# Two model blocks on one core: the second block's attention emitted in three stages per half head, across heads

## The chip, the cores and the metric

The kernel runs as one program on one core of a Trainium2 chip. The metric is the device time of that program in microseconds (us): the median of repeated runs. One further execution was recorded by the profiler. The rows shown in this document come from that recording, and their times count from the start of its span.

The engines are called PE (matrix engine; PEld is its loading of weights), DVE (vector), ACT (scalar activations), POOL (general) and SP (it issues the DMAs here).

## What is computed

The reference has two parts. The first (`first_block`, two layers of feed-forward, a mixer and feed-forward) is not touched by the change. The second is two layers of the function below, on 512 tokens of width 1024, with 16 heads of size 64:

```python
def hybrid_layer(x, mem, norm_g, w_in, w_out, mem_norm_g, w_mem_kv, qk_g):
    h = rms_norm(x, norm_g)
    proj = jnp.einsum('btd,de->bte', h, w_in)
    sizes = [D_MOBA] * 4 + [D_DIL] * 4 + [D_MEM] * 2
    cuts = [int(c) for c in np.cumsum(sizes)[:-1]]
    a_q, a_k, a_v, a_g, b_q, b_k, b_v, b_g, m_q, m_g = jnp.split(proj, cuts, axis=-1)

    qa = rope(rms_norm(to_heads(a_q, N_HEADS_MOBA), qk_g[0]))
    ka = rope(rms_norm(to_heads(a_k, N_HEADS_MOBA), qk_g[1]))
    oa = from_heads(moba_attention(qa, ka, to_heads(a_v, N_HEADS_MOBA)))
...
    ob = from_heads(dilated_attention(qb, kb, to_heads(b_v, N_HEADS_DIL)))

    mkv = jnp.einsum('bmd,de->bme', rms_norm(mem, mem_norm_g), w_mem_kv)
    m_k, m_v = jnp.split(mkv, 2, axis=-1)
...
    om = from_heads(memory_attention(qm, km, to_heads(m_v, N_HEADS_MEM)))

    y = jnp.concatenate([oa * jax.nn.silu(a_g), ob * jax.nn.silu(b_g), om * jax.nn.silu(m_g)], axis=-1)
    return x + jnp.einsum('bte,ed->btd', y, w_out)
```

There are 6, 6 and 4 heads of the three kinds, and 256 memory rows. With 512 tokens the kernel computes the first two kinds of attention as causal attention with one table added to the scores (a causal mask for a; for b a mask with the logarithm of how many of the patterns hold a key). Memory attention has no mask and 256 keys.

## The kernel before

*Precision.* Every operand of a matmul is held as two tiles, a rounded one (h, made on ACT by `hi`) and the residue (l, made by `lo` on DVE or POOL), and a product is three matmuls (`mm3`, lines 56 to 58). Weights come by DMA as `wf` and are split into `wh` and `wl`, three pieces ahead.

*Order.* The program is handed to a planner (`TileContext(nc, schedule_with_timeline_sim=True)`), which lays out each engine's instructions ahead of time along a modelled timeline. The order of emission is the priority; `high_priority(offset=n)` moves a stretch n instructions forward. An instruction whose operands or buffers are not free in the model lets later ones go first. On the chip each engine then runs its list strictly in that order, and waits where an operand is late. What is told below of places and order is the order of emission.

*Buffers.* Tiles with the same tag share a number of buffers. In PSUM: `acc` 3, `sc` 2 (scores), `tp` 2 (transposes), `o` 1 (weighted sums). In SBUF: `p` 3 (exponentials), `t` 6 (a scratch ring shared by `os`, `rx`, `sq`, `u`, `n`, `m`, `th`, `mf`, `mss`), `AH2`, `AL2`, `AH4`, `AL4` one each, `qk` 2, `v` 2, `gate` 4.

*A layer of the second block* (`hyb`). Eight pairs of heads are attended in the order of `PAIRS`; pairs 6 and 7 are the memory heads. Beside pair number pos the part `HYB[1 + pos]` is emitted as fill: u projects q and k of a pair (4 steps), v values of four heads (4), g a gate (2), m the memory's keys and values (4), and A, B, C are quarters of the output projection (4 each). `HYB[0]` comes ahead of the first pair, the last quarter behind the last. `blend` (line 569) steps through `attend` and after its i-th yield brings the fill up to the share i/n of its steps. Behind a unit u the products are turned into the layout of q and k by `turned`, two steps later.

*The attention of a pair* (`attend`, line 832 on). A pair has two heads h, and a head two halves (token blocks 0, 1 and 2, 3). For one half head:

- `scores` (838, 839): two matmuls for each block of 128 queries into `sc`; both blocks share a tile in the first half and for memory pairs, otherwise each has its own;
- `softmax` (824 to 829): on DVE the table is added and the minimum taken (scores are negated), on ACT the exponential with its sum into `l8`;
- transposes of `p` through `tp` (877 and 899), then `AH` on ACT and `AL` on DVE;
- `weighted` (846, 848): AH times (vh, vl) and AL times vh, accumulated in `po` (tag `o`). After the second half the two parts of `po` are added into `osum` (ACT, then DVE 912).

These four are emitted in one run. There is a yield behind each half and one between the two blocks of a second half, so a pair has 7 yields, and 5 in memory pairs. At a pair's end come 1/l (`rl` 915, `rx` 917, four transposes `pr` 920), two products with the gate (922, 923) and the split into `yh` and `yl`, which the output projection reads. A pair is finished before the next begins.

Of the kernel before, what the change touches and what calls it, by code (L numbers as in the profile page):

```python
# [11 lines left out]
F = _mybir.dt.float32  # L12
# [33 lines left out]
class Kernel:  # L46
# [532 lines left out]
    def hyb(self, l, hp, stats, after, late):  # L579
# [251 lines left out]
        def attend(pair, k):  # L831
# [20 lines left out]
            for h in range(2):  # L852
                head = 2 * pair + h
                hi_ = slice(64 * h, 64 * h + 64)
                po = self.ps.tile([P, T], F, tag="o", name="o", bufs=1)
                for half in range(2):
                    blocks = [(2 * half + ii, 2 if mem else 2 * half + ii + 1) for ii in range(2)]
                    if half == 0 or mem:
                        nb = sum(kn for _, kn in blocks)
                        sc = self.ps.tile([P, T], F, tag="sc", name="sc", bufs=2)  # L860
                        p = hp.tile([P, T], F, tag="p", name="p", bufs=3)
                        pt = self.ps.tile([P, T], F, tag="tp", name="pt", bufs=2)
                        o = 0
                        for i, kn in blocks:
                            e = o + kn * P
                            scores(sc[:, o:e], h, i, kn * P, o == 0, e == nb * P)
                            o = e
                        o = 0
                        for i, kn in blocks:
                            softmax(head, i, sc[:, o:o + kn * P], p[:, o:o + kn * P], l8[:, i, h:h + 1])  # L870
                            o += kn * P
                        o = 0
                        for i, kn in blocks:
                            for kt in range(kn):

                                to = kt * 2 + i % 2 if nb == 4 else kt + i
                                nc.tensor.transpose(pt[:, to * P:(to + 1) * P], p[:, o:o + P], self.ident)  # L877
                                o += P
                        AH = hp.tile([P, T], R, tag="AH2", name="AH", bufs=1)
                        AL = hp.tile([P, T], R, tag="AL2", name="AL", bufs=1)  # L880
                        n = nb * P
                        self.hi(AH[:, :n], pt[:, :n])
                        self.lo(nc.vector, AL[:, :n], pt[:, :n], AH[:, :n])
                        c = 256 * half
                        parts = [(0, slice(c, c + 256), AH[:, 0:256], AL[:, 0:256], half == 0, False),
                                 (1, slice(c + 512 - n, c + 256), AH[:, 256:n], AL[:, 256:n], False, half == 1)]
                    else:

                        AH = hp.tile([P, 7, P], R, tag="AH4", name="AH", bufs=1)
                        AL = hp.tile([P, 7, P], R, tag="AL4", name="AL", bufs=1)  # L890
                        for i, kn in blocks:
                            n = kn * P
                            sc = self.ps.tile([P, T], F, tag="sc", name="sc", bufs=2)
                            p = hp.tile([P, T], F, tag="p", name="p", bufs=3)
                            scores(sc[:, :n], h, i, n, True, True)
                            softmax(head, i, sc[:, :n], p[:, :n], l8[:, i, h:h + 1])
# [6 lines left out]
                            if i == 2:  # L903
                                yield
                        parts = [(3, slice(384, 512), AH[:, 0], AL[:, 0], False, False)]
                        for kt in range(3):
                            A = [A[:, 2 * kt + 1:2 * kt + 3].rearrange("p a b -> p (a b)") for A in (AH, AL)]
                            parts.append((kt, slice(256, 512), *A, False, kt == 2))
# [286 lines left out]
```

## Time and profile before

| | |
|---|---|
| median of 3 runs | 2488.4 us (2486.3 to 2491.72) |
| the profiled execution | 2487.4 us |
| its span, from first to last instruction | 2485.6 us |
| PE busy | 2419.5 us, 97% of the span |
| the second block | from about 1842 us to the end |

A busy time is a union of the recorded spans of an engine's instructions. Matmuls are pipelined and their recorded spans overlap, so PE that is busy all the time isn't PE at its peak. The granted clock (PEclk) is the share of the matrix engine's full clock; a mean of 0.89 over a stretch means that part of it ran at half the clock. A row of the list of waits says who waited, for whom, the sum of the idle time of the waiting engine in us, how often, and the longest.

### The profile page before, as it was taken

Reading aid. Unit: us, or ns where it says so; the run is one execution under the profiler, and the core shown is the slowest. Engines: PE = TensorE matmul, PEld = TensorE weight load, DVE = VectorE, ACT = ScalarE, POOL = GpSimd, SP = SyncE. Lnnn points to the kernel's source line nnn. Section 1 sums busy time; section 2 is a strip of 40 time slices with the busy share of each in tenths; the row PEclk is TensorE's granted clock in tenths of the full one; section 3 lists DMA queues with packets and bytes.
Section 4 is the critical chain, followed back from the end, with each engine's and each line's share of the span. In section 5 each row is a group of like instructions: output and inputs, shape, how many; then the busy total and the mean of one; then the engine's idle time right before and its main releaser. Section 6 shows DMA issues by size and latency. Waiting matters only on the chain.

```text
span 2485.6 us, 32583 instructions
## 1 busy us (share of the span) xinstructions
PE 2419.5 (97%) x12278; PEld 2046.9 (82%) x12278; DVE 968.8 (39%) x1721; ACT 1071.3 (43%) x2029; POOL 1305.0 (53%) x1018
## 2 busy tenths in 40 slices
PE   8999999999999999999999999999998999899998
PEld 6888888887888888888888888888887899788987
DVE  3111014773111011111115771111037688967888
ACT  4333335544333233333335653333345566555664
POOL 7676555537677556667556447766653122231121
PEclk9999999999999999999999999999999999989999
DMA  3332333222323333333332223333332221122212
GB/s 129 93 102 94 95 100 97 84 78 87 102 93 98 98 94 98 98 95 99 95 107 91 80 77 94 96 100 94 100 108 73 89 68 60 60 77 85 69 60 77
DMA packets 66975, 223.36 MB, mean 90 GB/s; under 512 B 7681, under 2 KB 10881, under 8 KB 66817
## 3 DMA queue, kind: packets, MB, share of 16 engines
q1 hardware_dynamic: 66816, 221.27, 28.7%
q8 instruction: 97, 1.59, 0.3%
q14 instruction: 62, 0.50, 0.1%
HBM read 219.14 MB, written 2.10 MB: 89 GB/s over the span
## 4 chain that ended last, share of the span: by engine, by line
PE 87%; DVE 8%; issue 2%; ACT 2%; POOL 2%; DMA 1%; SPq 0%; POOLq 0%; DVEq 0%; ACTq 0%
PE acc L56 20%; PE acc L57 20%; PE acc L58 20%; PE up L56 6%; PE up L58 6%; PE up L57 6%; DVE wl L67 1%; POOL ss L126 1%; PE sc L838 1%; PE o L846 1%; PE sc L839 1%; PE o L848 1%; DVE x L194 1%; DVE xl L114 1%; PE pt L877 1%
## 5 line engine op out<-in xcount | busy, mean ns | idle before, releaser
L67 POOL TENSOR_TENSOR wl<-wf,wh 128x512 fp32r<-128x512 f32 (+1 forms) x654 | 834.8, 1277 | 661.1 <-ACT wh L62 655.5
L62 ACT CAST wh<-wf 128x512 fp32r<-128x512 f32 (+1 forms) x814 | 497.5, 612 | 1110.4 <-PE acc L57 686.6
L56 PE MATMUL acc<-xh,wh 128*128 128x512 f32 x992 | 389.6, 393 | 6.5 <-ACT wh L62 6.0
L57 PE MATMUL acc<-xl,wh 128*128 128x512 f32 x992 | 389.4, 392 | 6.0 <-DVE xl L114 5.8
L58 PE MATMUL acc<-xh,wl 128*128 128x512 f32 x992 | 388.0, 391 | 0.1
L57 PE MATMUL up<-xl,wh 128*128 128x512 f32 x704 | 274.1, 389 | 0.0
L56 PE MATMUL up<-xh,wh 128*128 128x512 f32 x704 | 274.1, 389 | 0.0
L58 PE MATMUL up<-xh,wl 128*128 128x512 f32 x704 | 273.9, 389 | 0.0
L56 PE MATMUL acc<-hh,wh 128*128 128x512 f32 x704 | 273.9, 389 | 0.0
L57 PE MATMUL acc<-hl,wh 128*128 128x512 f32 x704 | 273.9, 389 | 0.0
L58 PE MATMUL acc<-hh,wl 128*128 128x512 f32 x704 | 273.9, 389 | 0.0
L57 PEld LDWEIGHTS acc<-xl,wh 128*128 128x128 f32 x992 | 186.7, 188 | 47.2 <-DVE xl L114 10.4
L57 PE MATMUL acc<-wl,xh 128*128 128x256 f32 (+1 forms) x752 | 220.7, 295 | 3.8 <-DVE wl L67 3.8
L56 PEld LDWEIGHTS acc<-xh,wh 128*128 128x128 f32 x992 | 186.8, 188 | 45.5 <-ACT wh L62 6.0
L58 PE MATMUL acc<-wh,xl 128*128 128x256 f32 (+1 forms) x752 | 220.3, 295 | 0.6 <-DVE xl L114 0.6
L56 PE MATMUL acc<-wh,xh 128*128 128x256 f32 (+1 forms) x752 | 216.5, 295 | 2.0 <-DVE v L704 1.6
L58 PEld LDWEIGHTS acc<-xh,wl 128*128 128x128 f32 x992 | 186.5, 188 | 38.3 <-POOL wl L67 0.9
L211 DVE TENSOR_TENSOR u<-up,R 128x512 f32<-128x512 f32 x88 | 60.8, 691 | 387.3 <-PE up L58 387.3
L209 DVE TENSOR_TENSOR g<-acc,R 128x512 f32<-128x512 f32 x88 | 60.9, 692 | 381.5 <-PE acc L58 381.4
L639 POOL TENSOR_TENSOR n<-u,ts 128x512 f32<-128x512 f32 x24 | 33.2, 1386 | 310.7 <-ACT u L635 310.4
L222 DVE SCALAR_TENSOR_TENSOR x<-acc,x 128x512 f32<-128x512 f32 x32 | 22.1, 692 | 389.4 <-PE acc L58 389.4
L58 PEld LDWEIGHTS acc<-hh,wl 128*128 128x128 f32 x704 | 132.1, 188 | 27.5
(235 smaller groups left out, 4372.4 us busy)
## 6 DMA issues: line engine op xcount, KB each, us to landing
wf<-wgu SPq DMA_DIRECT2D x175, 512.0 KB, 3.5
wf<-wdn SPq DMA_DIRECT2D x64, 512.0 KB, 3.5
wf<-w2u SPq DMA_DIRECT2D x28, 512.0 KB, 3.6
wf<-wdn SPq DMA_DIRECT2D x32, 384.0 KB, 3.1
wf<-wmi SPq DMA_DIRECT2D x20, 512.0 KB, 3.5
wf<-wmo SPq DMA_DIRECT2D x16, 512.0 KB, 3.6
wf<-w2g SPq DMA_DIRECT2D x16, 512.0 KB, 3.5
wf<-w2o SPq DMA_DIRECT2D x16, 512.0 KB, 3.5
```

What stands on the lines that cost most here:

```text
L56: mm(out, sh, mh, start=start, stop=False, **kw)
L57: mm(out, sh, ml, start=False, stop=False, **kw)
L58: mm(out, sl, mh, start=False, stop=stop, **kw)
L62: self.nc.scalar.copy(out, src)
L67: eng.tensor_tensor(out, src, hi.bitcast(F), op=ALU.subtract)
L114: nc.vector.scalar_tensor_tensor(xl, self.x[k], g, xh.bitcast(F), op0=ALU.mult, op1=ALU.subtract)
L126: eng.tensor_tensor(self.ss[:, :n], self.ss[:, :n], sq[:, :n], op=ALU.add)
L194: self.nc.vector.tensor_tensor(self.x[d], po, self.x[d], op=ALU.add)
L209: nc.vector.tensor_tensor(g, pg, Rb, op=ALU.mult)
L211: nc.vector.tensor_tensor(u, pu, Rb, op=ALU.mult)
L639: nc.gpsimd.tensor_tensor(by4(n), by4(u), si, op=ALU.mult)
L838: nc.tensor.matmul(sc, q[:, t], kh[:, :n], start=first, stop=False, skip_group_check=True)
```

## The change

A half head is taken apart into three stages. `begin` emits scores and softmax and returns two functions: `turn` (transposes, AH and AL) and `weigh` (the weighted sum, after the second half the sum into `osum`, and after the pair's last unit the gate product and the split). A dictionary `stage` that lives across pairs holds what the unit before left: `advance` calls the transposes of the unit before, yields, then the weighted sum of the one before that, and yields. So there are three yields a unit, 12 a pair, for memory pairs as well. The last unit's `turn` and `weigh` and the last but one's `weigh` are called in the next pair's part. Two more calls of `advance` follow the last pair. 1/l and its product with the gate move from the pair's end into `turn` of its last unit, ahead of its last weighted sum. AH and AL get a tile for the first half and one for the second; memory pairs, which had one for both, alternate. `blend` gets n = 12, and 17 for the last pair, in place of 7, 5 and 9.

```diff
--- before.py
+++ after.py
@@ -849,81 +849,109 @@
             osum = scratch("os")
             l8 = self.sp.tile([P, 4, 2], F, tag="l8", name="l8", bufs=2)
...
+            po = [None]
+            def begin(h, half):
                 head = 2 * pair + h
...
+                blocks = [(2 * half + ii, 2 if mem else 2 * half + ii + 1) for ii in range(2)]
+                both = half == 0 or mem
+                ps_ = []
+                if both:
+                    sc = self.ps.tile([P, T], F, tag="sc", name="sc", bufs=2)
+                    p = hp.tile([P, T], F, tag="p", name="p", bufs=3)
+                    nb = sum(kn for _, kn in blocks)
+                    o = 0
+                    for i, kn in blocks:
+                        e = o + kn * P
+                        scores(sc[:, o:e], h, i, kn * P, o == 0, e == nb * P)
+                        ps_.append((i, kn, sc[:, o:e], p[:, o:e]))
+                        o = e
+                    for i, kn, c, q in ps_:
+                        softmax(head, i, c, q, l8[:, i, h:h + 1])
+                else:
+                    for i, kn in blocks:
+                        n = kn * P
                         sc = self.ps.tile([P, T], F, tag="sc", name="sc", bufs=2)
                         p = hp.tile([P, T], F, tag="p", name="p", bufs=3)
...
+                        scores(sc[:, :n], h, i, n, True, True)
+                        softmax(head, i, sc[:, :n], p[:, :n], l8[:, i, h:h + 1])
+                        ps_.append((i, kn, sc[:, :n], p[:, :n]))
+                parts = []
+                def turn():
+                    AH = hp.tile([P, 4 + 3 * half, P], R, tag=f"AH{half}", name="AH", bufs=1)
+                    AL = hp.tile([P, 4 + 3 * half, P], R, tag=f"AL{half}", name="AL", bufs=1)
+                    if both:
+                        pt = self.ps.tile([P, 4, P], F, tag="tp", name="pt", bufs=2)
+                        for i, kn, _, p in ps_:
                             for kt in range(kn):
                                 to = kt * 2 + i % 2 if nb == 4 else kt + i
...
+                                nc.tensor.transpose(pt[:, to], p[:, kt * P:(kt + 1) * P], self.ident)
+                        self.hi(AH[:, :nb], pt[:, :nb])
+                        self.lo(nc.vector, AL[:, :nb], pt[:, :nb], AH[:, :nb])
                         c = 256 * half
...
+                        A2 = lambda f, t: tuple(flat(A[:, f:t]) for A in (AH, AL))
+                        parts.extend([(0, slice(c, c + 256), *A2(0, 2), half == 0, False),
+                                      (1, slice(c + 512 - nb * P, c + 256), *A2(2, nb), False, half == 1)])
                     else:
...
+                        for i, kn, _, p in ps_:
                             pt = self.ps.tile([P, 4, P], F, tag="tp", name="pt", bufs=2)
                             for kt in range(kn):
                                 nc.tensor.transpose(pt[:, (kt + i - 2) % 4], p[:, kt * P:(kt + 1) * P], self.ident)
                             ah, al = (A[:, 3 - i:7:2] for A in (AH, AL))
                             self.hi(ah, pt[:, :kn])
                             self.lo(nc.vector, al, pt[:, :kn], ah)
...
+                        parts.append((3, slice(384, 512), AH[:, 0], AL[:, 0], False, False))
                         for kt in range(3):
...
+                            parts.append((kt, slice(256, 512), *(flat(A[:, 2 * kt + 1:2 * kt + 3]) for A in (AH, AL)),
+                                          False, kt == 2))
+                    if h == 1 and half == 1:
+                        rl = self.sp.tile([P, 8], F, tag="rl8", name="rl8", bufs=2)
+                        nc.vector.reciprocal(rl, flat(l8))
+                        rx = scratch("rx").rearrange("p (a b) -> p a b", b=64)
+                        nc.vector.tensor_scalar(rx, rl.unsqueeze(2).to_broadcast([P, 8, 64]), 0.5, None, op0=ALU.mult)
+                        pr = self.ps.tile([P, T], F, tag="tp", name="pr", bufs=2)
+                        for i in range(4):
+                            nc.tensor.transpose(pr[:, i * P:(i + 1) * P], flat(rx[:, 2 * i:2 * i + 2]), self.ident)
+                        nc.vector.tensor_tensor(gates[pair], gates[pair], pr, op=ALU.mult)
+                def weigh():
+                    if half == 0:
+                        po[0] = self.ps.tile([P, T], F, tag="o", name="o", bufs=1)
+                    weighted(po[0], h, parts)
                     if half == 1:
...
+                        hi_ = slice(64 * h, 64 * h + 64)
+                        self.hi(osum[hi_], po[0][64:P])
+                        nc.vector.tensor_tensor(osum[hi_], po[0][0:64], osum[hi_], op=ALU.add)
+                        if h == 1:
+                            gt = gates[pair]
+                            nc.vector.tensor_tensor(gt, gt, osum, op=ALU.mult)
+                            y_tile(k)
+                            self.hi(yh[k], gt)
+                            self.lo(nc.vector, yl[k], gt, yh[k])
+                return turn, weigh
+            for h in range(2):
+                for half in range(2):
+                    new = begin(h, half)
                     yield
...
+                    yield from advance(new)
+        stage = {"turn": None, "weigh": None}
+        def advance(new):
+            old, w = stage["turn"], stage["weigh"]
+            if old is not None:
+                old[0]()
+            yield
+            if w is not None:
+                w()
+            stage["turn"], stage["weigh"] = new, old and old[1]
             yield
         def due(n):
@@ -950,9 +978,11 @@
             pass
         for pos, pair in enumerate(self.PAIRS):
             part = self.HYB[1 + pos]
-            n = 5 if pair >= 6 else 7
-            self.blend(attend(pair, pos), n + 2 if pos == 7 else n, steps(part), sum(self.STEPS[c[0]] for c in part.split()))
+            fill, m = steps(part), sum(self.STEPS[c[0]] for c in part.split())
+            main = attend(pair, pos)
+            if pos == 7:
+                main = itertools.chain(main, advance(None), advance(None))
+            self.blend(main, 17 if pos == 7 else 12, fill, m)
             if pos == 1:
                 late()
         for _ in self.out_part(yh, yl, 3, after):
```

## Rows read from the trace of the kernel before

**Rows 1.** Page, part 1: each engine's busy us (share of the span) xinstructions

```profile
PE 2419.5 (97%) x12278; PEld 2046.9 (82%) x12278; DVE 968.8 (39%) x1721; ACT 1071.3 (43%) x2029; POOL 1305.0 (53%) x1018
```

**Rows 2.** Stretches: us, busy of PE, PEld, DVE, ACT, POOL; clock; DMA share, GB/s

```profile
0.00:1842.00 1842.00, 1818.63 (x8319) 1508.46 (x8320) 460.92 (x753) 709.16 (x1238) 1165.79 (x927) 1.00 0.31 95
1842.00:2486.00 644.00, 600.90 (x3961) 538.48 (x3959) 507.86 (x968) 362.18 (x791) 139.18 (x91) 0.97 0.24 74
...
1903.00:1950.00 47.00, 34.60 (x179) 26.64 (x178) 34.18 (x69) 29.37 (x67) 15.14 (x14) 0.89 0.26 79
2220.00:2260.00 40.00, 32.51 (x150) 24.66 (x149) 30.80 (x62) 26.98 (x62) 13.28 (x12) 0.83 0.25 77
...
2430.00:2470.00 40.00, 38.84 (x202) 32.01 (x201) 38.13 (x73) 21.80 (x48) 8.88 (x5) 1.00 0.17 54
2180.00:2220.00 40.00, 40.00 (x302) 38.33 (x302) 27.34 (x55) 21.31 (x47) 9.62 (x6) 0.99 0.26 80
...
2380.00:2400.00 20.00, 16.50 (x107) 14.14 (x106) 15.45 (x36) 11.44 (x31) 6.06 (x4) 0.91 0.03 3
```

**Rows 3.** What PE waited for, 1842 to 2486: us in total, times, longest us

```profile
PE o L846 <- ACT AH L62: 5.2, 7, 1.1
PE acc L56 <- ACT mm L759: 4.8, 3, 2.6
PE o L846 <- DVE os L912: 4.6, 6, 1.4
PE o L848 <- DVE AL L67: 3.9, 6, 2.0
...
PE pr L920 <- DVE rx L917: 2.8, 2, 1.8
PE po L56 <- ACT yh L62: 2.7, 2, 1.4
...
PE pt L877 <- DVE AL L67: 1.5, 1, 1.5
```

**Rows 4.** The same in the memory stretches, 1903 to 1950, then 2220 to 2260

```profile
PE o L848 <- DVE AL L67: 2.0, 1, 2.0
PE o L846 <- DVE os L912: 1.8, 2, 1.4
...
PE o L846 <- ACT AH L62: 1.1, 1, 1.1
PE pr L920 <- DVE rx L917: 1.0, 1, 1.0
...
PE pr L920 <- DVE rx L917: 1.8, 1, 1.8
PE o L846 <- DVE os L912: 1.4, 1, 1.4
PE o L848 <- DVE AL L67: 0.8, 2, 0.4
PE o L846 <- ACT AH L62: 0.3, 1, 0.3
```

**Rows 5.** PE's timeline in the sixth pair: start us, us, instruction, [idle before]

```profile
2069.26 0.34 PE L838 MATMUL sc<-qk 128*128 128x384 f32 x1
...
2069.62 0.28 PE L846 MATMUL o<-AH,v 128*128 128x256 f32 x1
2069.74 0.28 PE L848 MATMUL o<-AL,v 128*64 128x256 f32 x1
```

**Rows 6.** What SP's queue waited for, 1842 to 2486: us, times, longest

```profile
SPq L755 <- DVE gate L814: 9.6, 1, 9.6
SPq L755 <- DVE rx L917: 6.5, 1, 6.5
...
SPq L755 <- DVE gate L923: 4.1, 2, 2.9
```

More of the change, by code (lines that the diff above doesn't have):

```diff
@@ L851, in attend @@
             l8 = self.sp.tile([P, 4, 2], F, tag="l8", name="l8", bufs=2)
-            for h in range(2):
+            po = [None]
+            def begin(h, half):
                 head = 2 * pair + h
[L854 to L859, printed above, removed]
+                blocks = [(2 * half + ii, 2 if mem else 2 * half + ii + 1) for ii in range(2)]
[16 more added lines that the diff above has]
+                        n = kn * P
@@ L860, in attend @@
                         sc = self.ps.tile([P, T], F, tag="sc", name="sc", bufs=2)
                         p = hp.tile([P, T], F, tag="p", name="p", bufs=3)
[L862 to L873, printed above, removed]
+                        scores(sc[:, :n], h, i, n, True, True)
+                        softmax(head, i, sc[:, :n], p[:, :n], l8[:, i, h:h + 1])
+                        ps_.append((i, kn, sc[:, :n], p[:, :n]))
+                parts = []
@@ L878, in attend @@
[L878 to L883, printed above, removed]
+                                nc.tensor.transpose(pt[:, to], p[:, kt * P:(kt + 1) * P], self.ident)
+                        self.hi(AH[:, :nb], pt[:, :nb])
@@ L884, in attend @@
+                        self.lo(nc.vector, AL[:, :nb], pt[:, :nb], AH[:, :nb])
                         c = 256 * half
-                        parts = [(0, slice(c, c + 256), AH[:, 0:256], AL[:, 0:256], half == 0, False),
-                                 (1, slice(c + 512 - n, c + 256), AH[:, 256:n], AL[:, 256:n], False, half == 1)]
-                    else:
[L889 to L896, printed above, removed]
+                        A2 = lambda f, t: tuple(flat(A[:, f:t]) for A in (AH, AL))
@@ L909, in attend @@
-                    weighted(po, h, parts)
-                    if half == 1:
-                        self.hi(osum[hi_], po[64:P])
-                        nc.vector.tensor_tensor(osum[hi_], po[0:64], osum[hi_], op=ALU.add)
-                    yield
-            rl = self.sp.tile([P, 8], F, tag="rl8", name="rl8", bufs=2)
-            nc.vector.reciprocal(rl, flat(l8))
-            rx = scratch("rx").rearrange("p (a b) -> p a b", b=64)
-            nc.vector.tensor_scalar(rx, rl.unsqueeze(2).to_broadcast([P, 8, 64]), 0.5, None, op0=ALU.mult)
@@ L918, in attend @@
-            pr = self.ps.tile([P, T], F, tag="tp", name="pr", bufs=2)
-            for i in range(4):
-                nc.tensor.transpose(pr[:, i * P:(i + 1) * P], flat(rx[:, 2 * i:2 * i + 2]), self.ident)
-            gt = gates[pair]
-            nc.vector.tensor_tensor(gt, gt, pr, op=ALU.mult)
-            nc.vector.tensor_tensor(gt, gt, osum, op=ALU.mult)
-            y_tile(k)
-            self.hi(yh[k], gt)
-            self.lo(nc.vector, yl[k], gt, yh[k])
+                            parts.append((kt, slice(256, 512), *(flat(A[:, 2 * kt + 1:2 * kt + 3]) for A in (AH, AL)),
+                                          False, kt == 2))
```

6 lines of the change are left out of this document (removed).

## The prediction

> **What bounds the kernel now.** I first read the totals of the page: the matrix engine (PE) is busy 97% of the span [rows 1], so only what lets PE idle or slows it can be won. Then the table by stretch [rows 2] splits the span at 1842 us, where the second block begins. Before it PE is busy 1818.6 of 1842.0 us; the change touches nothing there. In the second block it is busy 600.9 of 644.0 us at a mean granted clock of 0.97: 43.1 us idle, and some 0.03 x 644 = 19 us of clock. That is all there is to win, and it is not spread evenly. The stretch 2180 to 2220 shows no idle time. The stretches 1903 to 1950 and 2220 to 2260, where the memory keys and values (the step m) are projected beside the attention of the second pair, lose 12.4 and 7.5 us of PE and run at a clock of 0.89 and 0.83. The stretch 2380 to 2400 loses 3.5 us at 0.91 [rows 2].
>
> Third, the list of what PE waited for in the second block [rows 3]. Five of its rows are waits inside the attention: the weighted sum for its left part AH (5.2 us, 7 times), for the sums of the head before to leave the one buffer o (4.6 us, 6 times), for the residue AL (3.9 us, 6 times), the transposes of 1/l for rx (2.8 us, 2 times), a transpose for a buffer that AL had still to read (1.5 us, once). Together 18.0 us in 22 waits. They are the target. The same list for the two memory stretches alone [rows 4], with the one transpose wait of 1.5 us, which stands in the first of them, holds 7.4 us in 6 waits and 4.3 us in 5: 11.7 us in 11 of the 22. So only 6.3 us in 11 waits lie anywhere else.
>
> The rows understate a wait a little. A weighted matmul is shown as 0.28 us long, but in an unbroken run the next one starts 0.12 us after it [rows 5]. The record runs 0.16 us past the moment at which the next could have started, so I add 0.16 us to each wait.
>
> **The change, part by part.** It adds and removes no instruction and no transfer. The same scores, exponentials, transposes, AH, AL and weighted sums are emitted in another order, and an order of emission is all that the planner gets from the program. Before, a half head was emitted as one run (scores, softmax, transposes, AH and AL, weighted sum) with fill between half heads, at 7 places a pair (5 for the memory pairs). After, one unit's scores, the unit before's transposes and the one before that's weighted sum stand between 12 places a pair, and two stages of a pair's last unit, one of its last but one, fall into the next pair's part.
>
> *The stage distance.* From one stage of a unit to the next there are now four places for fill. The block takes 644 us for 16 pairs, so a pair has about 40 us, a place 3.4 us, four of them 13 us, as an estimate. The longest wait in these five rows is 2.0 us [rows 3]. So wherever PE has other ready work, these waits should go. Outside the memory stretches they are 6.3 + 11 x 0.16 = 8.1 us. I take 5.5 us, two thirds, because some of them stand at the end of a part, where the projections run out and the planner will pull stages forward again. Bounds: 0 and 8.1.
>
> *The memory stretches.* Here the waits are 11.7 + 11 x 0.16 = 13.5 us. They stand beside waits of PE for mm, the operand of the memory projection (4.8 us in 3 waits [rows 3]). The loads of memT that feed mm were held by the SP queue for tiles of the shared scratch ring t: 9.6 us until a gate had been computed, 6.5 us until rx, 4.1 us until the last product of a pair [rows 6]. So PE had little else to do, and a wait that is taken from the weighted sum is mostly handed on to the next operand. I take a quarter, 3.5 us, because with the new order three half heads are in flight and can fill each other's gaps. Bounds: 0 and 13.5.
>
> *The clock.* The granted clock is 0.89 over 47 us, 0.83 over 40 us and 0.91 over 20 us [rows 2]: 5.2 + 6.8 + 1.8 = 13.8 us of full-speed time, and PE is busy in about four fifths of it, so 11 us at most. The drops stand in the stretches with much idle time and follow it. If only a fifth to a quarter of that idle time goes, I take 2 us. Bounds: 0 and 11.
>
> *1/l moved forward.* rl, rx, the four transposes pr and the product with the gate now stand ahead of the last weighted sum, right behind the last seven transposes of p. On PE the pr transposes wait there for rx on the vector engine (DVE) and for one of the two buffers tp, and what is queued behind them is fill and the next weighted sum. Before, 2 of 16 pairs waited, 1.4 us each on average [rows 3]. Ends: all gone (-2.8) or all 16 pairs wait (16 x 1.4 = 22, so +20). Nearest is the row itself: I leave it at no change.
>
> *The end of a layer.* The last unit's product, its split yh and the last quarter of the output projection stand as before one behind the other. PE waited 2.7 us for yh in both layers together [rows 3]. The new order leaves two steps of fill behind the last weighted sum where the old one left five, but the products of the last quarter with the y of the pair before are there as cover in both. I take no change; bounds -3.0 and +3.0, the latter by one more wait like those in the row.
>
> *The scratch ring.* A pair's sum os is now held about five places into the next pair's part, and rx goes into that part too. Beside the second pair that part is the memory step, whose loads waited 4.1 us for the slot of os and 6.5 us for rx's computation already [rows 6]. Bounds: nothing, if the load takes a slot that was free anyway, and 4.1 + 6.5, about 11 us, if these waits double. I take 3 us.
>
> **Sum.** -5.5 - 3.5 - 2 + 3 = -8.0 us. The profiled execution took 2487.4 us (its span 2485.6), which gives 2479.4. It lies 1.0 us under the median of the runs, 2488.4, so on the median 2480.4; I forecast **2480**, with its own range from 2464 to 2483.
>
> **The rivals.** *The overlap is there already.* The planner doesn't keep the program's order. In the trace the scores for the second half of a pair's second head start at 2069.26 us, ahead of the weighted sum of its first head's first half at 2069.62 [rows 5]; so the stages of different half heads do run in one another's gaps already, as far as p, sc and tp have buffers, and the new order only moves the point at which the same shortage shows. Then the 18 us stay within a few and the time is 2488, from 2483 to 2493. For it: two thirds of the target stand where PE has no other work. Against: the 11 waits elsewhere.
>
> *Slower: the memory loads starve.* The loads of memT are issued in order by the SP queue together with the weights. If the planner gives scratch tiles to the finishing first pair (os, rx) ahead of memT, each of the two layers stands idle for about one more of those waits, 4.1 to 6.5 us, plus the clock that such idle time cost (6.8 us in 2220 to 2260 [rows 2], of which I count a third). That is 6 to 9 us a layer, 12 to 18 in all, less what the first two terms give (some 5): 2488 + 10 = **2498**. It decides as soon as the first memT load is issued later, counted from the last gate of the part before, than now.
>
> The Trainium skill has a rule that speaks against this change: Perfetto Trace Analysis, section Optimization Strategy, says that the same gap repeating on the engine that should be saturated can mean that there isn't enough SBUF or PSUM for the next tile. By that rule the wait for o, which has a single buffer, and the waits for scratch tiles come from buffer counts, which the change leaves as they are, and the time would be that of one of these two rivals. The trace agrees as far as the SP waits go; for o it shows only that the wait exists, and not that a later weighted sum would not miss it.
>
> *Much faster.* Everything in the first two terms goes and half of the clock: -8.1 - 13.5 - 5.5 = -27, which is 2461.
>
> The vector engine is no rival of its own, though it is busy 38.1 of 40 us in the stretch 2430 to 2470 [rows 2]. PE is busy 38.8 us there, and the change adds no work to either. If late stages of the pair before crowd it, PE waits for x or for yh, which the bound of the layer's end holds.
>
> **How the numbers follow.** A difference of 0.2% (5.0 us) is about what a measurement of this kernel can tell from no change. Chances: forecast (2464 to 2483) 0.42; overlap there already (2483 to 2493) 0.28; memory loads starve (2493 and above) 0.20; much faster (under 2464) 0.10. So faster 0.52, same 0.28, slower 0.20. The range from 2462 to 2498 leaves out about half of the last two cases, 0.08 on the low side and 0.10 on the high side.
>
> **What would show it.** In the profile after, PE's list of waits in the second block should have the rows of the weighted sum (AH, AL, os) down from 13.7 us to about 7, most of what is left in the memory stretches. The stretches beside the first and second pair should still idle and still show a clock under 0.95. The memory step's mm row should stay near 4.8 us; if it doubles, the slower rival holds. If the sum of the attention's rows falls and PE's idle time doesn't, the waits were handed on, and the first rival holds. I would be wrong altogether if waits appeared in stretches that show none now, as 2180 to 2220, or if the pr row grew tenfold.

## The result: 1.35% faster, and what the profile after shows

| | before | after |
|---|---|---|
| median of 4 runs | 2488.06 us (2486.3 to 2491.72) | 2454.46 us (2451.52 to 2456.68) |
| after / before | | 0.9865, 95% interval 0.9852 to 0.9879 |
| span of the profiled execution | 2485.6 us | 2453.7 us |

The kernel became 33.6 us faster where I forecast 8, and the time lies below my range. The profiled spans differ by 31.9 us. First the totals of the page after, which answer to [rows 1]: the same number of instructions on every engine.

```profile
PE 2404.0 (98%) x12278; PEld 2042.3 (83%) x12278; DVE 961.6 (39%) x1721; ACT 1069.5 (44%) x2029; POOL 1307.8 (53%) x1018
```

Next the kernel after by stretch (columns as in [rows 2]). The second block still begins at 1842 us. The boundaries of the four shorter stretches are the same instructions of PE in both kernels, to within 1 us. In each layer they are the first product behind the memory projection that waits for the memory's values v (called its end below), and the first product of the last quarter of the output projection that waits for yh. The third stretch begins with the second layer's first product that waits for its weights.

```profile
0.00:1842.00 1842.00, 1818.38 (x8323) 1507.72 (x8324) 457.93 (x753) 709.04 (x1238) 1167.26 (x928) 1.00 0.31 95
1842.00:2454.00 612.00, 585.61 (x3957) 534.61 (x3955) 503.69 (x968) 360.47 (x791) 140.56 (x90) 0.99 0.25 78
...
1842.00:1938.00 96.00, 88.85 (x583) 81.19 (x582) 74.43 (x145) 54.50 (x117) 30.70 (x22) 0.95 0.33 102
1938.00:2142.00 204.00, 200.92 (x1387) 183.95 (x1385) 173.91 (x342) 122.08 (x272) 36.80 (x21) 1.00 0.22 68
2160.00:2241.00 81.00, 74.53 (x496) 68.21 (x497) 61.97 (x123) 48.06 (x107) 26.67 (x20) 0.96 0.29 92
2241.00:2443.00 202.00, 200.05 (x1388) 184.19 (x1387) 170.99 (x333) 122.51 (x272) 37.28 (x21) 1.00 0.21 66
```

The same four stretches of the kernel before:

```profile
1842.00:1950.00 108.00, 94.37 (x605) 82.51 (x604) 77.28 (x153) 58.55 (x125) 29.48 (x23) 0.95 0.29 92
1950.00:2156.00 206.00, 199.96 (x1369) 181.89 (x1367) 172.70 (x333) 119.54 (x264) 37.62 (x22) 1.00 0.21 67
2174.00:2266.00 92.00, 83.24 (x514) 73.46 (x515) 65.02 (x131) 51.36 (x115) 25.84 (x20) 0.89 0.26 81
2266.00:2475.00 209.00, 202.21 (x1369) 183.66 (x1369) 170.69 (x324) 119.31 (x264) 37.10 (x22) 0.99 0.21 64
```

The first block is unchanged. The first and third rows, which run to the end of the memory projection, became 12 and 11 us shorter; the second and fourth 2 and 7 us. Not all of the 23 us is gain there: those two stretches hold 22 and 18 matmuls fewer, which the new order moved behind their end. At 204/1387 = 0.15 us each that is 5.9 us of moved work. So as an estimate some 17 of the 32 us were won up to the end of the memory projection in both layers, and 15 behind it.

By kind, over the second block: PE's idle time went from 2485.6 - 1842 - 600.9 = 42.7 us to 26.1, a gain of 16.6 us. Time at the lower of the clock's two levels (1.2 GHz; 2.4 is the full one), worked out as twice the missing share of the granted clock over short consecutive stretches, went from 37.5 to 19.3 us; at half speed that is 9.1 us of full-speed time. About 6 us are left. I put 3.5 of it on the ends of records (0.16 us for each of the 22 waits of the attention); the rest stays unassigned.

PE's list of waits from 1842 us on, after (columns as in [rows 3]):

```profile
PE acc L57 <- DVE wl L67: 4.7, 2, 2.6
PE pt L662 <- DVE m L650: 3.2, 2, 2.6
PE acc L56 <- ACT mm L759: 3.0, 2, 2.5
PE po L56 <- ACT yh L62: 2.7, 2, 1.4
PE sc L838 <- DVE qk L67: 2.5, 1, 2.5
...
PE o L848 <- DVE AL L67: 0.4, 1, 0.4
```

The five rows of the attention fell from 18.0 us in 22 waits [rows 3] to this last row, 0.4 us. So the intended effect is there in full. But it can't be the whole: 18.0 us of waits don't make 32 us. Two other rows came in their place: the transposes of q and k wait 3.2 us for m, where they waited 0.2 us before, and the scores 2.5 us for qk, a wait that the kernel before doesn't have.

The lead came from ACT's list at the place where the first large gap of the kernel before opens. Here is ACT's timeline of the kernel before (start us, us, instruction, [idle before it and for whom]). `sq` is the first step of q and k for the **second** pair (`normed`); it reads the product of the projection u that was emitted as fill beside the first pair. `os` is the copy of the **first** pair's weighted sum:

```profile
1903.84 0.62 ACT L62 CAST wh<-wf 128x512 fp32r<-128x512 f32 x1 [2.31 <-PE acc L57]
1904.62 0.58 ACT L62 COPY os<-o 64x512 f32<-64x512 f32 x1 [0.16 <-PE o L848]
1905.22 1.08 ACT L621 ACTIVATE sq<-acc 128x512 f32<-128x512 f32 x2
```

and of the kernel after:

```profile
1896.64 0.60 ACT L621 ACTIVATE sq<-acc 128x512 f32<-128x512 f32 x1
...
1897.89 0.59 ACT L621 ACTIVATE sq<-acc 128x512 f32<-128x512 f32 x1
...
1905.80 0.58 ACT L62 COPY os<-o 64x512 f32<-64x512 f32 x1 [0.54 <-PE o L848]
```

PE had finished that projection at the same time in both, to 0.5 us. (The first sq reads only the first of its two halves, so after it can start a little ahead of the last matmul.) Its last matmul, from PE's timeline of before and then of after:

```profile
1896.54 0.28 PE L58 MATMUL acc<-wh,xl 128*128 128x256 f32 x1
```

```profile
1897.04 0.28 PE L58 MATMUL acc<-wh,xl 128*128 128x256 f32 x1
```

So before, the product for q and k of the second pair lay ready for 8.4 us (1896.8 to 1905.2), because in ACT's list their first step stood behind a copy that had to wait for PE's weighted sum. ACT idled in that time, for 2.31 us at a stretch: that is the wait of a split of weights (wh) for PE, which stood ahead of the copy. After, the first sq starts 8.6 us earlier, and what hangs on it moves too: the first memT load goes from 1912.6 to 1907.3 us, the first scores of the second pair from 1923.1 to 1913.1, the end of the memory projection from 1949.7 to 1937.2.

### The profile page after: what moved, and what is told of

Same layout as the page of the kernel before. It is cut to its first block, busy times and chain, and to the rows that moved or that the text cites. A ratio compares the mean times of both kernels' runs of the same rounds, so it can differ in the third digit from the quotient of the medians.

```text
span 2453.7 us, 32584 instructions
## 1 busy us (share of the span) xinstructions
PE 2404.0 (98%) x12278; PEld 2042.3 (83%) x12278; DVE 961.6 (39%) x1721; ACT 1069.5 (44%) x2029; POOL 1307.8 (53%) x1018
## 4 chain that ended last, share of the span: by engine, by line
PE 89%; DVE 7%; issue 2%; POOL 1%; ACT 1%; DMA 1%; SPq 0%; POOLq 0%; DVEq 0%; ACTq 0%
PE acc L56 21%; PE acc L57 20%; PE acc L58 20%; PE up L58 6%; PE up L57 6%; PE up L56 6%; POOL ss L126 1%; PE pt L903 1%; DVE wl L67 1%; PE sc L838 1%; PE o L846 1%; PE sc L839 1%; PE o L848 1%; PE pt L891 1%; DVE xl L114 0%
## 5 line engine op out<-in xcount | busy, mean ns | idle before, releaser
L211 DVE TENSOR_TENSOR u<-up,R 128x512 f32<-128x512 f32 x88 | 60.8, 691 | 387.3 <-PE up L58 387.3
L56 PEld LDWEIGHTS up<-xh,wh 128*128 128x128 f32 x704 | 132.2, 188 | 27.6
```

Of the source, the lines that this page charges most:

```text
L56: mm(out, sh, mh, start=start, stop=False, **kw)
L211: nc.vector.tensor_tensor(u, pu, Rb, op=ALU.mult)
```

## Experiments

**Theory A, distance:** the stages' distance takes the waits away, and the rest follows from PE's idle time and clock. **Theory B, place of the fill:** the projection's follow-up work (sq and what comes behind it) moved ahead of the first pair's end. What puts it behind was open at first; after the first runs I formed **theory B'**: `os`, `sq`, `u`, `m` and `n` are tiles of one scratch ring `t` with six buffers. The planner may move instructions, but if a tag's buffers go out in order of emission, a sq emitted behind the first use of os can't get its buffer until os has had its own, and os is not written before PE's weighted sum is done.

By the order of emission, B' says this of the first pair. Beside a pair, a share of the fill decides before which place the projection's follow-up is emitted. In the kernel before, os is first used ahead of place 3 of 7 and the follow-up comes at place 5: sq behind os. In the kernel after, os is first used ahead of place 12 of 12 and the follow-up comes at place 8: sq ahead. The two kinds of lever below move the one past the other, or take os out of the ring.

All runs stood beside the kernel before on their chip (medians 2487.5, 2485.5 and 2487.1 us in the three groups). PE's idle time is the span less 1842 us less PE's busy time in the second block; half clock is worked out as above, and up to 2.1 us of each figure lie past the end of the span, as the last stretch at half clock runs on there. Both are of the one profiled execution. Each ratio has its own kernel before as base, so between groups the ratios are to be compared. `first sq` is that of the second pair of layer 0. `sq late` takes all the projections u1 to u6 of both layers (the number is that of the pair whose q and k they make): the time from PE's last product of a projection to the start of its first sq, where it is later, summed.

| kernel | order in emission | median us | ratio to before, 95% interval | first sq us | sq late us | PE idle us | half clock us |
|---|---|---|---|---|---|---|---|
| before | os, sq | 2488.06 | | 1905.2 | 85.7 | 42.7 | 37.5 |
| after | sq, os | 2454.46 | 0.9865 (0.9852 to 0.9879) | 1896.6 | 16.2 | 26.1 | 19.3 |
| no_lag | os, sq | 2484.24 | 0.9988 (0.9979 to 0.9997) | 1906.5 | 69.6 | 42.0 | 35.8 |
| old_fill_early | os, sq | 2486.92 | 0.9998 (0.9988 to 1.0007) | 1903.9 | 102.5 | 44.8 | 43.3 |
| fill_later | os, sq | 2468.95 | 0.9927 (0.9909 to 0.9944) | 1904.8 | 42.1 | 36.2 | 40.3 |
| lag_in_pair | sq, os | 2449.30 | 0.9850 (0.9836 to 0.9865) | 1894.0 | 20.0 | 24.1 | 7.0 |
| fill_late | sq, os | 2453.00 | 0.9862 (0.9846 to 0.9879) | 1898.8 | 0 | 25.6 | 15.1 |
| old_fill_first | sq, os | 2453.35 | 0.9861 (0.9846 to 0.9876) | 1893.3 | 16.2 | 22.0 | 21.6 |
| old_os_own | os out of the ring | 2447.82 | 0.9839 (0.9820 to 0.9859) | 1895.3 | 0 | 22.5 | 11.3 |
| no_lag_os_own | os out | 2450.03 | 0.9850 (0.9832 to 0.9869) | 1894.8 | 0 | 24.2 | 9.9 |
| lag_os_own | os out | 2448.68 | 0.9845 (0.9829 to 0.9862) | 1896.0 | 0.3 | 23.2 | 10.3 |
| after_os_own | os out | 2451.97 | 0.9855 (0.9840 to 0.9869) | 1896.3 | 0 | 22.8 | 20.5 |
| fill_later_os_own | os out | 2452.61 | 0.9862 (0.9847 to 0.9877) | 1899.0 | 0 | 24.4 | 18.3 |
| old_sq_out | sq out, u, m, n in | 2476.81 | 0.9958 (0.9942 to 0.9975) | 1900.7 | 0 | 37.3 | 29.8 |

`first sq` tells of one projection, `sq late` of all twelve. Counted through in the same way, the order of emission puts the sq of u6 behind os in all of the eight kernels that leave os and sq in the ring, those of u1 to u5 in before, no_lag and old_fill_early, those of u1 to u3 in fill_later, and that of u2 in lag_in_pair. In these kernels 39 of the projections have a sq more than 2 us late. Each of them is one that the emission puts behind os, and in ACT's list it starts 0.6 us behind the start of a copy of os (1.1 us for u2 in the kernel before). The others that are put behind it aren't late, since os had its value before their product was there. Where os or sq is out of the ring, none is more than 0.3 us late. The 16.2 us of the kernel after are u6, 8.1 us in each layer.

**1. The stages without distance (no_lag).** The kernel after, its places and its code, but each unit's transposes and weighted sum are emitted right behind its scores:

```diff
-                    yield from advance(new)
+                    new[0]()
+                    yield
+                    new[1]()
+                    yield
...
-            if pos == 7:
-                main = itertools.chain(main, advance(None), advance(None))
-            self.blend(main, 17 if pos == 7 else 12, fill, m)
+            self.blend(main, 15 if pos == 7 else 12, fill, m)
```

> The new kernel with the same twelve places a pair, but each unit's own transposes come at its next place and its own weighted sum at the one after (no lag behind the unit before, nothing carried into the next pair). If the finer places are the cause, 2455 to 2460. If the distance between the stages is the cause, one place of 3 us instead of four should bring back part of the waits: 2470 to 2480. If carrying the last unit into the next pair is the cause, about 2485. In every case the first layer's end of the memory step tells where it went: 1937 us after, 1950 before.

All but 0.12% of the gain is gone. The block by stretch and three rows of PE's waits:

```profile
1842.00:2482.80 640.80, 598.81 (x3965) 540.43 (x3964) 510.60 (x968) 362.10 (x792) 142.38 (x91) 0.97 0.24 75
```

```profile
PE o L848 <- DVE AL L67: 4.2, 5, 2.1
PE o L846 <- DVE os L928: 4.2, 5, 1.4
...
PE o L846 <- ACT AH L62: 3.4, 5, 1.1
```

Taken alone this speaks for theory A, or for carrying the last unit into the next pair, of which I had expected about 2485 (experiment 2 excludes that). But ACT's list has changed back with it:

```profile
1905.89 0.58 ACT L62 COPY os<-o 64x512 f32<-64x512 f32 x1 [0.49 <-PE o L848]
1906.49 1.09 ACT L621 ACTIVATE sq<-acc 128x512 f32<-128x512 f32 x2
```

Without the distance os is first used ahead of place 6, and the follow-up at place 8 is behind it again. One run took away two things; only the later ones part them.

**2. The distance within a pair alone (lag_in_pair).** No stage is carried into the next pair:

```diff
                     yield from advance(new)
+            yield from advance(None)
+            yield from advance(None)
...
-            self.blend(main, 17 if pos == 7 else 12, fill, m)
+            self.blend(main, 17 if pos == 7 else 16, fill, m)
```

> The new kernel with the lag kept, but each pair's last stages flushed at the pair's own end, sixteen places a pair. If the distance between the stages is the cause, within 5 us of the new kernel, 2452 to 2460. If the cause is that a pair's last unit is carried into the part of the next pair, where it covers the wait for the next q and k, most of the 34 us are lost again: 2475 to 2488.

The whole gain is there, at 2449.3 us even a little more than expected, so carrying work across pairs isn't its source.

**3. The fill moved (old_fill_early, fill_late).** In the kernel before the fill one place earlier, in the kernel after two places later:

```diff
-            while done < m * min(i + 1, n) // n:
+            while done < m * min(i + 2, n) // n:
```

```diff
-            while done < m * min(i + 1, n) // n:
+            while done < m * min(max(i - 1, 0), n) // n:
```

> The kernel before with one number changed: the fill of a pair is brought up one place earlier, so that the projection of the next pair's q and k ends earlier, as it does by 8.6 us in the trace of the new kernel. If that earlier end is the cause, the memory stretches shrink without any staging: 2465 to 2478. If the stages themselves are the cause: 2485 to 2492.

> The new kernel with the fill brought up two of twelve places later, so that the projections end later against the attention, and the rest of a part is emitted at the pair's end. If the earlier end of the projections is the cause, a good half of the gain is lost: 2470 to 2480, all of it in the memory stretches. If the distance between the stages is the cause, within 5 us of the new kernel: 2450 to 2460.

Neither did anything, as I had expected of theory A. Theory B, where the place itself counts, falls: moving it by a seventh or a sixth of a pair left the time where it was. What did stay the same in both is the order: place 4 is still behind the first use of os at place 3, place 10 still ahead of the one at place 12. That led to B'.

**4. os out of the ring (old_os_own).** The kernel before with its old order of emission, and a tile of its own for osum. The ring gives up one buffer for it, so no space is added:

```diff
-            return hp.tile([P, T], F, tag="t", name=name, bufs=6)
+            return hp.tile([P, T], F, tag="t", name=name, bufs=5)
...
-            osum = scratch("os")
+            osum = hp.tile([P, T], F, tag="os", name="os", bufs=1)
```

> The kernel before, its order of attention untouched, with the sums osum taken out of the scratch ring t into a tile of their own (t has 5 buffers in place of 6, so the space is the same). The ACT lists show why: in the kernel before the first squares sq of a projection stand directly behind osum's copy, which waits for PE, in most pairs; in the new kernel they stand ahead of it. If tiles of the shared ring are handed out in the order of emission, so that the projection's first step queues behind the attention's osum, this alone brings most of the gain: 2458 to 2470, the first squares of the second pair's projection at about 1897 instead of 1905 us. If the distance between the stages is the cause: 2483 to 2492.

These two lines, without any stages, give the whole gain, and more than the 2458 to 2470 that I expected: 2447.8 us, the fastest median of all these kernels, though its interval overlaps that of the kernel after. ACT's list has sq where PE's projection ends, as in the kernel after:

```profile
1895.27 0.60 ACT L621 ACTIVATE sq<-acc 128x512 f32<-128x512 f32 x1 [0.32 <-PE acc L58]
...
1896.88 0.60 ACT L621 ACTIVATE sq<-acc 128x512 f32<-128x512 f32 x1
...
1903.99 0.58 ACT L62 COPY os<-o 64x512 f32<-64x512 f32 x1 [0.42 <-PE o L848]
```

The attention's waits didn't quite go. The block by stretch, and three rows of PE's waits:

```profile
1842.00:2447.40 605.40, 582.87 (x3958) 531.70 (x3956) 501.95 (x968) 358.53 (x791) 142.18 (x91) 0.99 0.25 79
```

```profile
PE o L848 <- DVE AL L67: 3.3, 2, 3.0
...
PE o L846 <- DVE os L912: 0.6, 1, 0.6
...
PE o L846 <- ACT AH L62: 0.2, 1, 0.2
```

4.1 us of them are left against 0.4 with the stages, and yet the kernel is no slower. So most of the 18 us of waits went when q and k were no longer late. That PE had stood at the weighted sums because it had no other work ready fits this, but no row here shows it directly; experiment 6 comes nearer.

**5. The distance with os out of the ring (no_lag_os_own, lag_os_own, later after_os_own).** The two lines of experiment 4 on no_lag, on lag_in_pair and on the kernel after; in each:

```diff
+            return hp.tile([P, T], F, tag="t", name=name, bufs=5)
...
+            osum = hp.tile([P, T], F, tag="os", name="os", bufs=1)
```

> The no-lag order with its twelve places, with the same separate tile for osum. If the ring's order is the cause, as fast as the kernel before with that tile or a little faster: 2455 to 2470. If the distance is the cause, as without that tile: 2480 to 2488.

> The lag within a pair with the separate tile for osum. If the ring's order is the whole cause, this is no faster than the lag within a pair (2449): 2446 to 2453. If lag and tile each remove waits of their own, a few us faster: 2440 to 2446.

> The new kernel, with its last stages carried into the next pair, and the separate tile for osum. If the ring's order is all that the change repaired, no faster than the kernel before with that tile (2448): 2446 to 2455; above 2452 the carrying costs a few us.

With os out of the ring the old order, three stages without distance, distance within the pair and distance across pairs lie at 2447.8, 2450.0, 2448.7 and 2452.0 us, their intervals overlapping. no_lag went from a ratio of 0.9988 to 0.9850 by these two lines alone, below the range that I expected. The distance as such is worth nothing that these runs can measure.

**6. sq put behind os again (fill_later, fill_later_os_own).** The kernel after with the fill five places later, so that the follow-up beside the first pair comes at the pair's end, behind the use of os ahead of place 12; then the same with os out of the ring:

```diff
-            while done < m * min(i + 1, n) // n:
+            while done < m * min(max(i - 4, 0), n) // n:
```

> The new kernel with the fill brought up five of twelve places later, so that a projection's end is emitted behind the pair's first use of osum, as in the kernel before; the lag between the stages stays. If the ring's order is the cause, a good part of the gain is lost: 2465 to 2485, and sq stands behind os again. If the distance is the cause: 2450 to 2460.

> The new kernel with the late fill that cost it 14 us (2469), and the separate tile for osum. If the ring's order was what the late fill brought back, the time returns to 2446 to 2456. If the late fill costs by itself, 2464 to 2472.

ACT's list turns over beside the first pair, with all stages and their distance in place:

```profile
1904.22 0.58 ACT L62 COPY os<-o 64x512 f32<-64x512 f32 x1 [0.38 <-PE o L848]
1904.83 1.09 ACT L621 ACTIVATE sq<-acc 128x512 f32<-128x512 f32 x2
```

and nearly half of the gain is lost: 0.73% is left of 1.35%. With os out of the ring it is back (1.38%): it was the order against os, not the late fill. That only half was lost where no_lag loses nearly all has its reason in the order too: u1 and u3 are 4 of the 6 steps of their parts, but u4 and u5 are 4 of 8, and five places later their follow-up comes at place 11, still ahead of os's first use. ACT's list has u3 behind os, and u4 and u5 as soon as their products are there:

```profile
2041.67 0.58 ACT L62 COPY os<-o 64x512 f32<-64x512 f32 x1 [1.11 <-PE o L848]
2042.28 1.09 ACT L621 ACTIVATE sq<-acc 128x512 f32<-128x512 f32 x2
...
2058.27 0.60 ACT L621 ACTIVATE sq<-acc 128x512 f32<-128x512 f32 x1
...
2092.11 0.58 ACT L621 ACTIVATE sq<-acc 128x512 f32<-128x512 f32 x1
...
2093.88 0.58 ACT L62 COPY os<-o 64x512 f32<-64x512 f32 x1 [0.28 <-PE o L848]
```

So 42.1 us of late sq came back where no_lag has 69.6 and the kernel before 85.7. The starts of the same products agree: against its twin with os out of the ring, no_lag loses some 16 us up to the last product of the memory projection, in both layers together, and 20 us behind it; fill_later loses 11 us and 5 us. And with the attention's waits nearly gone, PE's list names q and k (m), and the memory's operand that comes behind them, as what PE stands at:

```profile
PE acc L56 <- ACT mm L759: 9.7, 4, 6.7
PE pt L662 <- DVE m L650: 9.1, 2, 7.6
```

These rows hold 3.0 and 3.2 us in the kernel after.

**7. One number (old_fill_first).** The kernel before with the fill three places earlier, so that the follow-up stands ahead of the first use of os:

```diff
-            while done < m * min(i + 1, n) // n:
+            while done < m * min(i + 4, n) // n:
```

> The kernel before, ring and order of attention untouched, with the fill brought up three places earlier, so that a projection's end is emitted ahead of the pair's first use of osum. If the ring's order is the cause, most of the gain comes from this one number: 2452 to 2468, sq ahead of os in the ACT list. If the separate tile helped for another reason (one more buffer, another address), 2482 to 2490.

It gives 2453.35 us, the time of the kernel after, where one place earlier (old_fill_early) gave nothing. Between the two lies the point at which sq passes os; two places were not tried.

**8. sq alone out of the ring (old_sq_out).** In the kernel before only sq gets a tag of its own; u, m and n, which follow it, stay in the ring behind os:

```diff
-                sq = scratch("sq")
+                sq = self.sp.tile([P, T], F, tag="sq", name="sq", bufs=2)
```

> The kernel before with the first square of the projection's steps taken out of the ring (into a tile of another tag that is free in this block), while its u, m and n and osum stay in the ring. If each tile of the ring queues behind osum, sq goes ahead but the next steps still wait: a part of the gain, 2455 to 2480. If only the ring's number of tiles matters: 2482 to 2490.

A third of the gain (2476.8 us): sq comes 4.5 us earlier (1900.7), and the next step, u, still stands directly behind os:

```profile
1900.71 0.60 ACT L621 ACTIVATE sq<-acc 128x512 f32<-128x512 f32 x1 [0.27 <-PE acc L58]
...
1909.58 0.58 ACT L62 COPY os<-o 64x512 f32<-64x512 f32 x1 [0.44 <-PE o L848]
1910.19 0.59 ACT L635 COPY u<-acc 128x512 f32<-128x512 f32 x1
```

Summed as `sq late` is, but to the start of the first copy into the tile u, the projections u1 to u5 are 60.8 us late here, 95.4 in the kernel before and 12.5 in the kernel after. This separates B' from a plain preference of the planner for os.

What stays open: I saw the engines' lists, not the planner at work. That buffers of a tag go out in order of emission is inferred from which order comes out in these kernels (four with os first, four with sq first, five with os out of the ring, and old_sq_out between), all of them as B' says, and from the 39 late projections, none of them where B' has sq ahead. A ring with a seventh buffer, the other way to ask whether its size matters, wasn't tried; old_os_own gets its gain with one buffer fewer in the ring.

## Why the prediction was right on the direction and wrong on the size

**What bounds the kernel.** Right: PE is the bound, and what can be won is its idle time and clock in the second block, with the largest share at the memory stretches. I then took the list of PE's waits for the target. A list of waits names what PE stood at, not what would have filled the gap. The view that would have told is the timeline of ACT at 1905 us, which I did not read.

**Stage distance (-5.5).** Its sign held as a row: the waits went, more fully than forecast (0.4 us left where I wrote about 7). As a cause it fails: no_lag_os_own without any distance is as fast as the kernel after. Idle time in the two stretches behind the memory projection fell by (206.0 - 199.96) - (204.0 - 200.92) = 3.0 us and by 6.8 - 2.0 = 4.8 us, 7.8 in all, near my bound of 8.1; old_os_own, without any stages, gets more (3.7 us of idle time are left in these two stretches, where the kernel after has 5.0). Behind the memory projection, too, q and k had been late: the sq of u2 to u5 by 2.7 to 13.8 us.

**Memory stretches (-3.5). This is the step that failed.** I argued that PE had little else to do there, so that a wait taken away is handed on, and took a quarter of 13.5 us. I took the lack of work as given. It was the thing that changed: the work on q and k of the next pair began 8.6 us earlier, in layer 0, where PE had finished their projection all the same. Measured there: 17 us in both layers as worked out above, beyond even my upper bound of 13.5 for the waits, because the bound held the waits alone and not the late work behind them or the clock. The handing on itself is there: PE now waits 5.7 us for m and qk, that is for q and k, in place of 0.2.

**Clock (-2).** Also too small: 9.1 us came back, of my bound of 11. I had tied it to a fifth of the idle time; of 42.7 us of idle time 16.6 went, two fifths, and more than two fifths of the half-clock time with it.

**1/l moved (0) and the end of a layer (0).** Right. No wait of the transposes pr for rx is left (2.8 us before [rows 3]), and yh still costs 2.7 us in 2 waits.

**Scratch ring (+3).** The right object with the wrong sign. I asked who holds a slot longer (os, rx) and so delays the memory loads. I didn't ask in which order the slots go out, and who stands behind os that needn't. The wait for mm, which I had expected to stay or to double, fell from 4.8 to 3.0 us.

**The rivals.** "The overlap is there already" describes no_lag (2484.2 against 2488 forecast for that rival) and, in a way that I hadn't seen, the whole change: the distance alone is worth nothing measurable. "Much faster" (2461, chance 0.10) was nearest to the result, but as a sum of the same terms it had the wrong cause too. "The memory loads starve" went the other way: the first memT load came 5.3 us earlier. The rule cited there (the Trainium skill, Perfetto Trace Analysis, section Optimization Strategy: a repeating gap on the engine to be saturated can mean too little room for the next tile) pointed at the right place. By it I gave the time of one of two rivals, since the change leaves the counts of buffers as they are. The runs say why that fell: what this ring of six costs depends on which of its tiles is emitted first, and the change turned that order round. In old_os_own the gain comes with no room added.

**Signs.** The stretches beside the first pairs still idle, as forecast; they still lose clock, but their mean is 0.95 and 0.96 in the rows above and not under 0.95. None of the failing signs came, except one in part: in 2180 to 2220, which showed no idle time before, PE now idles 5.3 us, but that is the gap beside the second pair of layer 1, which now comes earlier in the span (2206 to 2216 in place of 2220 to 2260), not a new one.

## What to carry to other kernels

When instructions of independent work share a tag, ask in which order its buffers are given out, and whether a step that is ready stands behind one that has to wait for another engine; a tile of its own for the long-waited one can be worth more than a new order, here 38 us of 2485.5 with two lines and no more space. Before costing a stall by its waits, find the work that would have filled it and follow that work back, on its own engine's timeline, to why it was late. And a run that takes a change away must be read for what else it takes away: no_lag alone would have spoken for the wrong theory.

## What the runs showed of the clock

Beside the second pair of layer 0 the granted clock fell only after PE had idled for some us, and was still down when PE was busy again. Kernel before, by stretch, around the gap (PE idles 5.3 us in the second row at 0.84, and 1.5 us in the third at 0.65):

```profile
1896.00:1904.00 8.00, 8.00 (x47) 6.75 (x47) 3.93 (x9) 3.94 (x9) 0.00 (x0) 1.00 0.30 79
1904.00:1914.00 10.00, 4.70 (x29) 3.42 (x28) 8.68 (x14) 5.27 (x10) 6.69 (x4) 0.84 0.16 55
1914.00:1924.00 10.00, 8.53 (x28) 6.41 (x28) 7.28 (x11) 6.95 (x14) 1.99 (x3) 0.65 0.14 42
```

and of the kernel after:

```profile
1890.00:1910.00 20.00, 16.83 (x116) 15.03 (x114) 16.37 (x37) 13.41 (x33) 8.24 (x5) 1.00 0.28 87
1910.00:1920.00 10.00, 9.46 (x36) 7.79 (x37) 8.84 (x18) 7.66 (x19) 0.73 (x1) 0.66 0.26 63
```

After, PE idles 3.2 us in the first row at the full clock, and is then busy 9.46 of 10 us at 0.66, about two thirds of it at 1.2 GHz. Nor does the half-clock time follow from the sum of idle time: old_fill_first idles 22.0 us and has 21.6 us at half clock, lag_in_pair idles 24.1 and has 7.0. By this alone two executions with like idle time can lie (21.6 - 7.0)/2 = 7 us apart; the difference of 8.0 us between the spans of the kernel after (19.3 us, 2453.7) and lag_in_pair (7.0 us, 2445.7) is mostly that, 6.2 us. But one kernel differs with itself in the same way: the four runs of the kernel after go from 2451.5 us at a mean clock of 0.998 to 2456.7 us at 0.995. The profiled run of lag_in_pair is the shortest of its four (2447.5 us), that of the kernel after the second longest (2455.5 us), and the medians lie 5.2 us apart. So the half clock of one execution is not a fixed property of its kernel. What decides it in a gap stayed open.
